# The branch output projections take their PSUM banks from the projections' pair instead of the attention scores' three

## The chip, the cores and the metric

One core of a Trainium2 chip runs the whole program once. The metric is the device time of one execution in microseconds (us); the median of several runs counts.

## The reference, cut to what matters

Two layers of a diffusion backbone work on 256 latent and 256 context tokens of width 1024. In each layer a combined input projection feeds four token mixers (differential attention, a Hyena long convolution, a Conformer convolution, latent attention). Their outputs are projected to the model's width branch by branch, gated and added, and projected once more; a mixture of 16 experts follows.

```python
def merge_branches(ys, g, p):
    gates = jax.nn.sigmoid(g.reshape(*g.shape[:-1], N_BRANCH, D_MODEL))
    acc, start = 0.0, 0
    for i, (y, w) in enumerate(zip(ys, BRANCH_WIDTHS)):
        acc = acc + gates[..., i, :] * (y @ p['w_branch'][start:start + w])
        start += w
    return acc @ p['w_out']
```

The change concerns `y @ p['w_branch']`, one product for each of the four branches. The last layer computes it for the latent tokens alone, so its tiles are 256 wide where those of layer 0 are 512.

## The kernel before

Every product of the mixers is an fp32 product made of three fp32r matmuls (`mm3`, lines 355 to 357): high by high, high by low and low by high parts, all accumulated in one PSUM bank of 128x512 fp32.

The eight banks are dealt out by four small pools. A bank is given to a new tile when all readers of the tile that held it last are done, and TensorE (PE), which works strictly in the order of the program, waits for that at the first matmul of the new tile.

- `pm`, two banks: the input projections with the gates (`body` in `stream`), the output projection, later the experts' first product.
- `psc`, three banks: the attention scores, the branch projections, the Hyena transforms, later the experts' second product.
- `px`, one bank, and `pt`, two banks: attention outputs and transposes.

A generator stands for each strand of work (`stream`, `hyena`, `mla`, `diff`, four `branch` strands, the expert loader). A planner, `Order.run`, records their instructions in one order that it works out from estimated costs. The banks are not part of its estimates. Where a strand yields, another can put its work in between.

Two properties matter here. A projection of the "t" kind, a gate above all, takes its bank once and is accumulated in pieces: in layer 0 of 4 of the 8 steps of k (`PIECE = (4, 2)`: two pieces of 12 matmuls), in layer 1 of 2 steps (four pieces of 6 matmuls). Between the pieces other strands run and the bank stays held. A gate tile is read by ScalarE (ACT), which writes tanh of it to `tg` (line 984).

A `branch` strand makes eight tiles of 128 output columns, two for each 256 columns of weights. A tile is 6 matmuls for three of the branches and 12 for the branch of the differential attention (`nk` is 2 or 4). It is read by VectorE (DVE), which multiplies it by the gate (line 1051 for the first branch that arrives, line 1054 for the others). DVE also works in the order of the program: score maxima (1272), attention weights (1506, 1507), the low parts of weights (349), the Conformer's taps (1230), the modulation's products (521) stand before and after these evictions. A weight's low part on DVE (line 349) waits for its high part, which ACT casts (line 348).

The expert loader issues the weights of the experts (`we`) on the queue of SyncE (SP), each as soon as one of twelve large SBUF buffers is free. The mixers use these buffers as well (`wi` raw weights, `wq` split weights, `uh` and `ul` the tokens), so the loader is held until projections and output projection give them back.

Of the kernel before, what the change touches and what calls it, by code (L numbers as in the profile page):

```python
# [213 lines left out]
def _a(n):  # L214
    return 0.19 + n / 1200


def _d(n):
    return 0.07 + n / 960


def _q(n):
    return 0.1 + n / 480
# [3 lines left out]
def kernel(ctx: ExitStack, tc: tile.TileContext, x, ctxt, cols, skip, lamb, fng, ta, tb, tcn, td,  # L227
# [23 lines left out]
    def ps(tag, bufs):  # L251
        return psum.tile([128, 512], F32, name=tag, tag=tag, bufs=bufs)

    def pm():
        return ps("pm", 2)

    def psc():
        return ps("psc", 3)
# [7 lines left out]
    def big(name, dt=F32):  # L266

        S.used += 1
        assert S.used <= NB, name
        return work.tile([128, 2048], dt, name=name, tag="big", bufs=NB)  # L270
# [4 lines left out]
    def room(n=1, low=False):  # L275
        return lambda: S.used + n + (S.kept if low else 0) <= NB

    def t2(name, dt=F32, w=512):
        return work.tile([128, w], dt, name=name, tag="t2", bufs=NT2)
# [66 lines left out]
    def split(hi, lo, src, eng=nc.vector):  # L346

        nc.scalar.copy(hi, src)  # L348
        eng.tensor_tensor(lo, src, hi.bitcast(F32), op=OP.subtract)  # L349

    def mm3(out, terms, first=True, last=True):

        n = len(terms)
        for i, (lh, ll, rh, rl) in enumerate(terms):
            nc.tensor.matmul(out, lh, rh, start=first and i == 0, stop=False)  # L355
            nc.tensor.matmul(out, lh, rl, start=False, stop=False)  # L356
            nc.tensor.matmul(out, ll, rh, start=False, stop=last and i == n - 1)  # L357
# [39 lines left out]
    def layer(l):  # L397
# [319 lines left out]
        def acc(k):  # L717
            n = len(accs)
            return accs[k % n][:, k // n * TQ:(k // n + 1) * TQ]
# [271 lines left out]
        def two(name):  # L991

            if last:
                t = t2(name + "hl", F32R)
                return t[:, :TQ], t[:, TQ:]
            return t2(name + "h", F32R), t2(name + "l", F32R)

        def branch(i, os, k0, ready, early):
            nk = len(os)
            ws, arr = {}, {}  # L1000

            def load(d2):
                if d2 < 4:
                    ws[d2] = []
                    for k in range(0, nk, 2):
                        w = t2("wbr")
                        nc.sync.dma_start(w.rearrange("p (k c) -> p k c", k=2),
                                          w_branch[l, (k0 + k) * 128:(k0 + k + 2) * 128].rearrange("(k p) c -> p k c", p=128)
                                          [:, :, d2 * 256:(d2 + 1) * 256])
                        ws[d2].append(w)  # L1010
                    arr[d2] = S.load(nk * 0.125)

            def cut(d2):
                bs = []
                for w in ws.pop(d2):
                    hi, lo = t2("wbrh", F32R), t2("wbrl", F32R)
                    split(hi, lo, w)
                    bs.append((hi, lo))
                return bs

            CUT = {"act": nk / 2 * _a(512), "dve": nk / 2 * _d(512)}
            yield early
            for d2 in range(BA[l]):
                load(d2)
            yield ready
            if not accs:
                yield from S.until(room(ns))
                accs.extend(big("acc") for _ in range(ns))
            yield tg_ev[i, 0]
            yield arr[0]  # L1030
            bs = cut(0)
            ready = yield CUT
            for d2 in range(4):
                yield tg_ev[i, 2 * d2]
                yield ready
                load(d2 + BA[l])
                if i == 0 and d2 == 2:
                    br_ev.t = 0.0
                for m in range(2):
                    kd = d2 * 2 + m  # L1040
                    yield tg_ev[i, kd]
                    p = psc()
                    mm3(p[:, :TQ], [tuple(b[:, (k % 2) * 256 + m * 128:(k % 2) * 256 + (m + 1) * 128] for b in bs[k // 2])
                                    + os[k] for k in range(nk)])
                    a = acc(kd)
                    g = tg.pop((i, kd))
                    tg_n[0] -= 1
                    acc_n[kd] += 1
                    PE = {"pe": nk * 3 * TQ * 0.00042, "dve": _d(TQ)}
                    if acc_n[kd] == 1:  # L1050
                        nc.vector.scalar_tensor_tensor(a, g, 1.0, p[:, :TQ], op0=OP.add, op1=OP.mult)
                        yield PE
                    else:
                        nc.vector.scalar_tensor_tensor(g, g, 1.0, p[:, :TQ], op0=OP.add, op1=OP.mult)
                        if acc_n[kd] < 4:
                            nc.gpsimd.tensor_tensor(a, a, g, op=OP.add)
                            yield {**PE, "pool": _q(TQ)}
                        else:
                            nc.vector.tensor_tensor(a, a, g, op=OP.add)
                            yield {**PE, "dve ": _d(TQ)}  # L1060
                    if acc_n[kd] == 4:
                        ac[kd] = two("a")
                        split(ac[kd][0], ac[kd][1], a)
                        acc_ev[kd].t = yield {"act": _a(TQ), "dve": _d(TQ)}
                    if m == 0 and d2 < 3:
                        yield arr[d2 + 1]
                        nxt = cut(d2 + 1)
                        ready = yield CUT
                if d2 < 3:
                    bs = nxt  # L1070
# [547 lines left out]
        if l == 0:  # L1618
            gens += [lambdas(), residual()]
        gens += [hyena(), mla(), rope("k"), rope("q"), diff(),  # L1620
                 branch(1, o_hy, 4, hy_done, k_ev), branch(2, o_cf, 6, cf_done, cfa_ev[1][0]),
                 branch(3, o_ml, 8, ml_done, ml_mid), branch(0, o_df, 0, df_done, df_mid)]
        mv = products([(l, 1), (l, 2)] + ([] if last else [(l + 1, 0)]), (1,) if last else (0, 1), lat_ev if last else u_ev)
        mv_at = MVP[l]
# [518 lines left out]
```

## Time and profile before

| | us |
|---|---|
| median of 3 runs | 1992.57 (1991.23 to 1993.66) |
| the profiled execution, whole | 1990.53 |
| its span in the trace | 1988.7 |
| PE busy | 1699.1 (85%) |
| DVE busy | 974.7 (49%) |
| ACT busy | 461.8 (23%) |
| mean granted clock of TensorE | 0.919 |

The program has four stages: the mixers of layer 0 up to about 660 us, the experts of layer 0 up to about 1130 us, the mixers of layer 1 up to about 1520 us, the experts of layer 1 to the end. The branch projections run from 205.0 to about 604 us and from 1338.3 to about 1484 us. A busy share says little across stages: PE leads in the mixers, the transfers of weights in the experts. Matmuls overlap, so a matmul of 0.39 us (128x512) starts every 0.23 us, and one of 0.28 us (128x256) every 0.12 us.

### The profile page before, as it was taken

The numbers are of one execution on the slowest core, as the hardware profiler recorded it, in microseconds if no ns is written. First come the engines' busy times: TensorE is split into PE (matmuls) and PEld (weight loads), VectorE is DVE, ScalarE is ACT, GpSimd is POOL, SyncE is SP. The second block draws the span as 40 slices with busy tenths as digits, with TensorE's granted clock in tenths as the row PEclk, the third lists the DMA queues.
The fourth block names the chain that finished last, engine by engine and source line by source line (L and its number), as shares of the span: only waits on it lengthen the run. The fifth ranks groups of instructions, "written<-read, shape, count | busy, mean of one in ns | idle before, by whom it ended". The sixth has DMA issues, their size and how long they took to land.

```text
span 1988.7 us, 27943 instructions
## 1 busy us (share of the span) xinstructions
PE 1699.1 (85%) x11132; PEld 1101.6 (55%) x11132; DVE 974.7 (49%) x2057; ACT 461.8 (23%) x933; POOL 219.7 (11%) x229
## 2 busy tenths in 40 slices
PE   5899999888989799899898788998997767767665
PEld 2677788666769634343332277888986423322222
DVE  4787789877774311222332285887864111111012
ACT  4423233334332100010100163344442000000001
POOL 1332021031101000000000042410210000000000
PEclk9899999899989899999999998999998977777677
DMA  8525334422436799999999944565659999999997
GB/s 282 169 86 167 128 117 134 148 90 85 133 128 241 277 381 413 416 417 416 414 417 415 393 149 154 176 197 167 209 208 367 413 415 414 412 414 412 414 414 274
DMA packets 206554, 550.72 MB, mean 277 GB/s; under 512 B 14102, under 2 KB 94168, under 8 KB 176600
## 3 DMA queue, kind: packets, MB, share of 16 engines
q1 hardware_dynamic: 206424, 548.94, 73.4%
q8 instruction: 88, 1.44, 0.3%
q14 instruction: 42, 0.34, 0.0%
HBM read 547.83 MB, written 1.05 MB: 276 GB/s over the span
## 4 chain that ended last, share of the span: by engine, by line
PE 50%; DMA 27%; DVE 12%; issue 6%; ACT 4%; POOL 1%; SPq 1%; ACTq 0%; DVEq 0%; POOLq 0%
DMA we<-in_w_ei_dram 13%; PE pm L1963 11%; DMA we<-in_w_eo_dram 8%; PE pm L355 7%; PE pm L357 7%; PE pm L356 7%; PE psc L1988 4%; DMA h<-in_w_eo_dram 3%; DVE wq L349 2%; PE psc L1852 2%; PE psc L355 2%; PE psc L357 2%; PE psc L356 1%; DVE aw L521 1%; DMA h<-in_w_ei_dram 1%
## 5 line engine op out<-in xcount | busy, mean ns | idle before, releaser
L1963 PE MATMUL pm<-we,xe 128*32 128x256 f32 (+1 forms) x2912 | 402.7, 537 | 101.2 <-DMA we<-in_w_ei_dram 99.4
L1963 PEld LDWEIGHTS pm<-we,xe 128*32 128x32 f32 (+1 forms) x2912 | 135.3, 135 | 346.2 <-issue 183.0
L355 PE MATMUL pm<-uh,wq 128*128 128x256 f32 (+1 forms) x832 | 290.8, 349 | 2.2 <-ACT u L819 1.9
L356 PE MATMUL pm<-ul,wq 128*128 128x256 f32 (+1 forms) x832 | 281.5, 338 | 1.0 <-POOL ul L828 1.0
L357 PE MATMUL pm<-uh,wq 128*128 128x256 f32 (+1 forms) x832 | 281.1, 338 | 0.0
L1975 DVE SCALAR_TENSOR_TENSOR ea<-ea,pm 128x512 f32<-128x512 f32 (+1 forms) x32 | 17.7, 554 | 428.5 <-ACT ea L1974 428.5
L349 DVE TENSOR_TENSOR wq<-wi,wq 128x1024 fp32r<-128x1024 f32 x131 | 166.9, 1285 | 78.7 <-ACT wq L348 78.3
L1988 PE MATMUL psc<-we,eaT 128*32 128x256 f32 (+1 forms) x1280 | 172.1, 513 | 34.2 <-DMA we<-in_w_eo_dram 34.2
L355 PEld LDWEIGHTS pm<-uh,wq 128*128 128x128 f32 x832 | 161.0, 193 | 23.9 <-issue 5.2
L356 PEld LDWEIGHTS pm<-ul,wq 128*128 128x128 f32 x832 | 161.2, 194 | 17.4 <-POOL ul L828 1.2
L357 PEld LDWEIGHTS pm<-uh,wq 128*128 128x128 f32 x832 | 160.8, 193 | 16.5
L2000 DVE TENSOR_TENSOR ye<-psc,modr 32x512 f32<-32x512 f32 (+1 forms) x120 | 66.4, 553 | 202.1 <-PE psc L1988 200.7
L348 ACT CAST wq<-wi 128x1024 fp32r<-128x1024 f32 x132 | 136.1, 1043 | 11.7 <-DMA wi<-in_w_in_dram 10.3
L1988 PEld LDWEIGHTS psc<-we,eaT 128*32 128x32 f32 (+1 forms) x1280 | 58.9, 130 | 141.9 <-issue 75.7
L1974 ACT ACTIVATE ea<-pm 128x512 f32<-128x512 f32 (+1 forms) x32 | 15.7, 491 | 482.2 <-PE pm L1963 482.2
L1230 DVE SCALAR_TENSOR_TENSOR ca<-up,colt,ca 128x510 f32<-128x510 f32 (+29 forms) x120 | 81.0, 675 | 2.2
L2032 ACT COPY eaT<-pt 128x512 f32<-128x512 f32 (+1 forms) x32 | 15.3, 479 | 277.7 <-PE pt L2030 277.7
L521 DVE SCALAR_TENSOR_TENSOR aw<-aw,h 128x512 f32<-128x512 f32 x96 | 77.4, 807 | 3.4
L1276 ACT ACTIVATE e<-psc,nm 128x512 f32<-128x512 f32 (+1 forms) x72 | 44.4, 618 | 147.7 <-DVE nm L1274 145.5
L355 PE MATMUL pm<-wq,uh 128*128 128x256 f32 (+1 forms) x240 | 71.7, 299 | 4.4 <-DVE rsq L319 1.6
L356 PE MATMUL pm<-wq,uh 128*128 128x256 f32 (+1 forms) x240 | 69.6, 290 | 0.0
L357 PE MATMUL pm<-wq,ul 128*128 128x256 f32 (+1 forms) x240 | 69.6, 290 | 0.0
(409 smaller groups left out, 2646.3 us busy)
## 6 DMA issues: line engine op xcount, KB each, us to landing
we<-in_w_ei_dram SPq DMA_DIRECT2D x233, 1024.0 KB, 14.3
we<-in_w_eo_dram SPq DMA_DIRECT2D x110, 1024.0 KB, 14.6
wi<-in_w_in_dram SPq DMA_DIRECT2D x58, 1024.0 KB, 5.4
aw<-in_ada_t_dram SPq DMA_DIRECT2D x160, 256.0 KB, 5.4
we<-in_w_ei_dram SPq DMA_DIRECT2D x52, 256.0 KB, 8.1
wbr<-in_w_branch_dram SPq DMA_DIRECT2D x40, 256.0 KB, 5.6
h<-in_w_ei_dram SPq DMA_DIRECT2D x40, 256.0 KB, 16.3
h<-in_w_eo_dram SPq DMA_DIRECT2D x40, 256.0 KB, 16.2
```

The lines of the kernel that those rows point to most:

```text
L348: nc.scalar.copy(hi, src)
L349: eng.tensor_tensor(lo, src, hi.bitcast(F32), op=OP.subtract)
L355: nc.tensor.matmul(out, lh, rh, start=first and i == 0, stop=False)
L356: nc.tensor.matmul(out, lh, rl, start=False, stop=False)
L357: nc.tensor.matmul(out, ll, rh, start=False, stop=last and i == n - 1)
L521: nc.vector.scalar_tensor_tensor(o, wt_, 1.0, cb[s, k], op0=OP.mult, op1=OP.mult, accum_out=ends[lm, g][0][:, s, c, k:k + 1])
L1230: nc.vector.scalar_tensor_tensor(o, up[:, :, max(d, 0):256 + min(d, 0)], cw[:, c0 + d:c0 + d + 1], o, op0=OP.mult, op1=OP.add)
L1276: nc.scalar.activation(e, p[:, :nk], AF.Exp, scale=scale, bias=nm, accum_out=s)
L1852: nc.tensor.matmul(p[:, kk * n:(kk + 1) * n], h[2 * s + b][k // 4][:, (k % 4) * 128:(k % 4 + 1) * 128], hot[:, 2 * i + b], start=b == 0, s ...
L1963: nc.tensor.matmul(dst[j * M:(j + 1) * M, :], lhs, w[o + j * FW // 512][:, j * FW % 512:j * FW % 512 + FW], start=k == 0, stop=k == KC - 1 ...
L1988: nc.tensor.matmul(py[j * M:(j + 1) * M, :FW], aT[:, c * 128 + q * M:c * 128 + (q + 1) * M], w[f % 2 * 2 + j * FW // 512][:, j * FW % 512: ...
L2000: nc.vector.tensor_tensor(ye[eg][s][c0 // 512][e4 * CAP:(e4 + 1) * CAP, c0 % 512:c0 % 512 + FW], py[r0:r0 + CAP, :FW], mod5[r0:r0 + CAP, c ...
```

## The change

One line in `branch` asks the other pool for the tile:

```diff
-                    p = psc()
+                    p = pm()
                     mm3(p[:, :TQ], [tuple(b[:, (k % 2) * 256 + m * 128:(k % 2) * 256 + (m + 1) * 128] for b in bs[k // 2])
                                     + os[k] for k in range(nk)])
```

The planner does not know of banks, so every engine's instructions stand in the order in which they stood. What differs is the tile that 480 matmuls (64 tiles of 6 or 12) write and their evictions read, and with it who waits for whom. PE in the tail of layer 1's mixers, before; the names end in tile numbers, `pm_11817` is a gate in its pieces, `psc_11840` and `psc_11849` are tiles of two branches:

```order
L357 MATMUL pm_11817<-uh_7856,wq_11550 128x256
L355 MATMUL psc_11840<-ohl_11516,wbrh_11754 128x256
L356 MATMUL psc_11840<-ohl_11516,wbrh_11754 128x256
L357 MATMUL psc_11840<-ohl_11516,wbrl_11755 128x256
L355 MATMUL psc_11840<-ohl_11527,wbrh_11754 128x256
L356 MATMUL psc_11840<-ohl_11527,wbrh_11754 128x256
L357 MATMUL psc_11840<-ohl_11527,wbrl_11755 128x256
L355 MATMUL psc_11849<-ohl_9732,wbrh_11674 128x256 [waits DVE_49]
```

The same place with the change, where the waits are those for the banks' last readers:

```order
L357 MATMUL pm_11817<-uh_7856,wq_11550 128x256
L355 MATMUL pm_11840<-ohl_11516,wbrh_11754 128x256 [waits Activation_49]
L356 MATMUL pm_11840<-ohl_11516,wbrh_11754 128x256
L357 MATMUL pm_11840<-ohl_11516,wbrl_11755 128x256
L355 MATMUL pm_11840<-ohl_11527,wbrh_11754 128x256
L356 MATMUL pm_11840<-ohl_11527,wbrh_11754 128x256
L357 MATMUL pm_11840<-ohl_11527,wbrl_11755 128x256
L355 MATMUL pm_11849<-ohl_9732,wbrh_11674 128x256 [waits DVE_49]
```

No instruction moved. The gate `pm_11817` is open across both tiles and holds one bank of the pair, so `pm_11840` has to wait for the other one, which ACT reads as the gate before it, and `pm_11849` for DVE's eviction of `pm_11840`. Before, `psc_11849` waited for the eviction of a tile three places back.

## Rows read from the trace of the kernel before

**Rows 1.** The page's first line.
```profile
span 1988.7 us, 27943 instructions
```
**Rows 2.** Windows: stretch, its length, busy PE PEld DVE ACT POOL, PEclk, DMA share, GB/s.
```profile
330.00:605.00 275.00, 243.73 (x1182) 191.63 (x1181) 210.49 (x466) 98.10 (x196) 39.67 (x38) 0.93 0.38 124
605.00:660.00 55.00, 55.00 (x472) 55.00 (x472) 19.77 (x43) 12.76 (x37) 9.98 (x14) 1.00 0.55 198
660.00:1130.00 470.00, 428.69 (x2002) 167.36 (x2003) 125.62 (x248) 39.50 (x80) 8.02 (x11) 0.97 1.01 405
1333.00:1420.00 87.00, 79.61 (x613) 75.08 (x612) 72.06 (x146) 41.26 (x78) 10.80 (x12) 0.96 0.60 192
1444.00:1486.00 42.00, 38.58 (x314) 37.57 (x313) 28.67 (x52) 18.61 (x35) 7.67 (x10) 1.00 0.50 173
1520.00:1985.00 465.00, 322.08 (x3340) 138.45 (x3340) 69.44 (x170) 22.36 (x58) 3.69 (x4) 0.77 0.99 399
```
**Rows 3.** Waits of PE, 320 to 605 us: total, times, longest.
```profile
PE psc L355 <- ACT e L1276: 8.4, 4, 6.2
```
**Rows 4.** Waits of PE, 1333 to 1486 us: total, times, longest.
```profile
PE psc L355 <- ACT e L1276: 6.1, 2, 3.1
```
**Rows 5.** Matmuls on branch weights: count, ns min/median/max, first and last start, forms.
```profile
L355 PE MATMUL psc<-oh,wbrh x80: 389/389/795, 205.0 to 603.5; 128*128 128x512 f32 x80
L355 PE MATMUL psc<-ohl,wbrh x80: 278/283/387, 1338.3 to 1483.8; 128*128 128x256 f32 x80
```
**Rows 6.** Timeline at 490 us, PE, ACT, DVE: start, us, idle before.
```profile
490.33 0.50 PE L355 MATMUL psc<-oh,wbrh 128*128 128x512 f32 x1 [0.64 <-ACT e L1276]
...
489.50 0.69 ACT L1276 ACTIVATE e<-psc,nm 128x512 f32<-128x512 f32 x1 [4.45 <-DVE nm L1274]
...
490.11 0.68 DVE L1054 SCALAR_TENSOR_TENSOR tg<-tg,psc 128x512 f32<-128x512 f32 x1
```
**Rows 7.** Timeline at 254 us, PE and ACT.
```profile
253.74 0.39 PE L355 MATMUL pm<-uh,wq 128*128 128x512 f32 x1
...
254.21 0.59 ACT L984 ACTIVATE tg<-pm 128x512 f32<-128x512 f32 x1
```
**Rows 8.** Timeline at 526 us, PE and DVE.
```profile
525.57 0.39 PE L355 MATMUL pm<-uh,wq 128*128 128x512 f32 x1
...
528.56 0.68 DVE L1054 SCALAR_TENSOR_TENSOR tg<-tg,psc 128x512 f32<-128x512 f32 x1
```
**Rows 9.** Timeline at 1340 us, PE and ACT.
```profile
1339.76 0.28 PE L355 MATMUL pm<-uh,wq 128*128 128x256 f32 x1
...
1342.03 0.38 ACT L984 ACTIVATE tg<-pm 128x256 f32<-128x256 f32 x1
```
**Rows 10.** Timeline at 1360 us, PE and DVE.
```profile
1359.30 0.28 PE L355 MATMUL pm<-uh,wq 128*128 128x256 f32 x1
...
1363.24 0.39 PE L355 MATMUL psc<-ohl,wbrh 128*128 128x256 f32 x1 [3.06 <-ACT e L1276]
...
1363.08 0.41 DVE L1051 SCALAR_TENSOR_TENSOR acc<-tg,psc 128x256 f32<-128x256 f32 x1
```
**Rows 11.** Timeline at 1474 us, PE, DVE, ACT.
```profile
1474.04 0.28 PE L355 MATMUL psc<-ohl,wbrh 128*128 128x256 f32 x1
...
1476.36 0.69 DVE L349 TENSOR_TENSOR wbrl<-wbr,wbrh 128x512 fp32r<-128x512 f32 x1
1476.97 0.75 DVE L1054 SCALAR_TENSOR_TENSOR tg<-tg,psc 128x256 f32<-128x256 f32 x2
```
**Rows 12.** Windows behind the wait of 3.06 us, columns as in rows 2.
```profile
1363.00:1365.00 2.00, 1.76 (x12) 1.76 (x13) 1.96 (x6) 1.99 (x6) 0.00 (x0) 0.86 0.01 3
1365.00:1368.00 3.00, 3.00 (x16) 3.00 (x16) 2.16 (x4) 0.83 (x3) 0.00 (x0) 0.52 0.33 87
```
**Rows 13.** Waits of SP's queue, 590 to 670 us.
```profile
SPq L1690 <- PE pm L357: 23.2, 4, 12.6
```
**Rows 14.** Waits of SP's queue, 1470 to 1530 us.
```profile
SPq L1690 <- PE pm L357: 19.2, 5, 6.2
```

## The prediction

> **What bounds the kernel now.** I read the windows first, stage by stage, then PE's waits, then the timeline where the branch projections stand. PE leads in both mixer stages: it is busy 243.7 of the 275 us up to 605 us, 79.6 of 87 us from 1333 us and 38.6 of 42 us from 1444 us, while DVE is busy 210.5, 72.1 and 28.7 us of these [rows 2]. In the two expert stages the transfers lead: a DMA share of 1.01 over 470 us and 0.99 over 465 us [rows 2]. Before each of these stages the share is only 0.55 and 0.50 [rows 2], because the expert loader's issues wait for PE's last reads of the mixers' buffers [rows 13, 14]. So a microsecond that PE loses in a mixer stage starts the stream of expert weights a microsecond later, and a stream at a share of 1 has nothing with which to catch up. The question is what PE loses or gains between 205 and 605 us and between 1333 and 1486 us.
>
> **What falls away.** No instruction is added, removed or moved on any queue, SP's and POOL's among them. The branch tiles leave the three score banks, and the waits for those banks go. PE waits for the exponentials of score tiles 8.4 us in four places of layer 0 and 6.1 us in two of layer 1 [rows 3, 4]. That is the most that can be gained, 14.5 us, if nothing took their place.
>
> **What comes in.** A gate holds one of the two banks over all its pieces, with branch tiles put in between; these then share the single bank left, and a tile must wait until DVE or ACT has read its predecessor. A branch tile passes quickly: six matmuls at a start every 0.23 us are 1.4 us in layer 0, at 0.12 us 0.7 us in layer 1 (the matmuls themselves last 0.389 and about 0.283 us and overlap [rows 5]). The eviction itself takes 0.4 to 0.7 us, but stands in DVE's queue behind other work. So I set, for each tile of the pair in the new deal of banks, the end of the predecessor's reader in this trace against the tile's own start. PE takes up a released bank 0.14 us after the reader's end: the exponential ends at 489.50 + 0.69 = 490.19 and PE starts at 490.33 [rows 6]. With that, 53 of the 134 tiles in the three stretches would start too early: 14 in layer 0 by 14.8 us together, 19 between 1333 and 1420 us by 31.6 us, 20 between 1444 and 1486 us by 36.8 us. Five show the kinds:
>
> - At 490.33 us the second tile of a pair follows its gate's first piece. It waited for the exponential until 490.19; now for DVE's eviction of the first tile, which ends at 490.11 + 0.68 = 490.79 [rows 6]. One wait replaces another, 0.6 us longer. This recurs at 502.07 us, and longer at 477.05 us.
> - At 253.74 us a gate gets the bank of the gate before last, which ACT reads until 254.21 + 0.59 = 254.80 [rows 7]: 1.2 us.
> - At 525.57 us a gate follows a branch tile whose eviction ends at 528.56 + 0.68 = 529.24 [rows 8]: 3.8 us.
> - At 1339.76 us a gate needs what ACT reads until 1342.03 + 0.38 = 1342.41 [rows 9]: 2.8 us.
> - At 1474.04 us a tile needs the bank that DVE frees behind a weight's low part, 1476.97 plus about 0.41, so 1477.38 [rows 11]: 3.5 us.
>
> The ends of the cost: if every eviction moved on rigidly with PE, each overshoot would be paid in full and the sum would be 14.8 + 31.6 + 36.8 = 83 us. If no eviction moved at all, only the largest of each stretch would be paid, 3.8 at 525.57, 4.3 at 1359.30 and 3.8 at 1478.40 us: 12 us, less waits that shrink. Neither holds: an eviction moves by as much as the work for which its queue waited had moved, and often this work lies before the stall. So I carried the delay on, stall by stall, along the waits of the program, each eviction kept at its distance behind the latest thing it waited for in the trace.
>
> *Layer 0*, nine places: 1.2 (253.74), 1.3 (397.65), 0.5 (466.16), 1.5 (477.05), 0.65 twice (490.33, 502.07), 1.4 (515.71), 2.8 (525.57), less 0.85 of a wait on a transpose bank soon behind it that shrinks, and 1.0 (578.70). Sum 10.2 us. A further 0.6 at 411 us is given back at 424 us, where PE waits for something else.
>
> *Layer 1, 1333 to 1420 us*: 2.9 (1339.76), 0.8, 0.7, 2.8 (1359.30), 1.0 (1376.84), 0.2, 1.5, 2.2, 0.7, 0.7, together 13.5. The stall at 1359.30 us, where the bank is free only at 1363.08 + 0.41 = 1363.49 [rows 10], lies right before a wait of 3.06 us that ended with an exponential [rows 10]; this wait vanishes and three small ones shrink behind the new stalls, which gives back 5.1. Net 8.4 us.
>
> *Layer 1, 1444 to 1486 us*: 0.9, 2.0, 1.7, 1.8, 1.1, 2.4 (1474.04), 0.2, 1.8 and some smaller ones, together 12.3; waits for weights' low parts and the one ahead of the output projection shrink by 4.0. Net 8.3 us.
>
> The sum is 10.2 + 8.4 + 8.3 = 26.9 us, against ends of 12 and 83. It is nearer to the lower end because most banks are freed behind work that does not depend on the stalled tile, as at 1474 us.
>
> **A rule weighed against the rows.** The wait of 3.06 us at 1363 us [rows 10] left its mark on the clock: granted 0.86 in the two microseconds behind it and 0.52 in the three after that [rows 12], so mostly the lower level, 1.2 of 2.4 GHz; that took 0.14 x 2 + 0.48 x 3 = 1.7 us. The Trainium skill, TensorE: Matmul & The Clock Gate, section "A second HAM failure mode: psum-queue depth-cycling", reports of a kernel that went round its PSUM banks and idled shortly between groups of matmuls that its clock kept switching, which cost throughput. By the rows no stall under 3 us is priced so, and the sum stays 26.9. By that rule the new stalls would each be followed by a slow stretch; the trace before cannot show it, and it is a rival below.
>
> **The rivals.** *The clock falls too.* If each of the 15 or so stalls of 1 us and more were followed by a slow stretch of 1.7 us [rows 12], 25 us more; if only the four of about 2.4 us and more, 7 us: 1990.5 + 26.9 + 7 = 2024, plus the 2 us below, 2026. For it: the stalls are close to each other in the tail of layer 1. Against: the clock stood at 1.00 over 1444 to 1486 us [rows 2], though PE idled 3.4 us there. The section of the Trainium skill named above is the rule of this rival. *The stream of weights takes it up.* If the loader's issues did not wait for the mixers' end, the expert stages would hide what layer 0 loses, and the time would be some 2009. Against: rows 13 and 14. *It gets faster.* The exponential waits go (14.5 us) and the evictions come before the exponentials that they follow now: 1992.6 - 14.5 = 1978. It decides at 490 us: the eviction would have to end before 490.19; it stands behind the second maximum and ends at 490.79 [rows 6]. *Nothing changes*, since evictions that are late here come in time once PE is a little later: 1992.6. Against: the nine places of layer 0 are each a wait for DVE or ACT work that begins after PE has delivered, so it moves with PE. That the change does not do what it says can be left out: the order of instructions shows all 64 tiles in the other pool.
>
> **How the numbers follow.** The profiled execution took 1990.53 us (a span of 1988.7 us [rows 1] and 1.8 us around it); 1990.5 + 26.9 = 2017.4. The median of the three runs is 2.0 us above it, so 2019. A measurement of this kernel can tell about 0.2%, 4 us, from no change. Chances: this forecast 0.72, within some 8 us either way for the carrying (2011 to 2027); the clock 0.12 (2024 to 2044); hidden in part 0.08 (2000 to 2010); nothing 0.03; faster 0.05. The range runs from 2007 to 2029: it leaves out the last two cases, most of the hidden one and the upper part of the clock's. Slower by over 0.2%: 0.92; within: 0.03; faster: 0.05.
>
> **What would show it.** In the profile of the changed kernel PE's waits for exponentials at the branch projections are gone or nearly so, and waits of line 355 for `tg` of lines 1054 and 984 stand in their place, some 40 to 55 us in all. The output projection of layer 0 begins about 10 us later, that of layer 1 about 27 us later; the expert stages last as long as before, at the same DMA share. Wrong would be the sum if the waits came to less than 25 us, the carrying if the delay at 605 us were under 6 or over 15 us, and the passing on if an expert stage were shorter.

## The result and the profile after

The changed kernel takes 2020.1 us (median of five runs, 2017.3 to 2023.0) against 1991.2 us for the kernel before in the same session (1987.2 to 1993.7): a ratio of 1.0146, 95% interval [1.0131, 1.0161], so 26 to 32 us slower. The forecast was 2019, from a sum of 26.9 us. The profiled execution of after took 2019.85 us, and its span is 29.4 us longer than before's. The page's first line and its line of engines:

```profile
span 2018.1 us, 27921 instructions
PE 1708.7 (85%) x11132; PEld 1104.9 (55%) x11132; DVE 972.7 (48%) x2057; ACT 463.0 (23%) x933; POOL 217.5 (11%) x229
```

The five engines have as many working instructions as before (PE 11132); the total is lower by 22, all of them instructions that only wait for semaphores. The span grew, and the next rows say where. They are the groups of branch matmuls by form, the counterpart of [rows 5]: count, ns min/median/max, first and last start in us, shape.

```profile
L355 PE MATMUL pm<-oh,wbrh x80: 389/395/796, 206.4 to 615.3; 128*128 128x512 f32 x80
L355 PE MATMUL pm<-ohl,wbrh x80: 277/283/582, 1350.4 to 1516.5; 128*128 128x256 f32 x80
```

The four starts are 1.4, 11.8, 12.1 and 32.7 us later than in [rows 5]. From the first to the last branch tile layer 0 lost 10.4 us. Between the layers, where the experts of layer 0 run, the delay stayed nearly as it was (11.8, then 12.1), and layer 1 added 20.6 us, of which 1.3 came back right behind the last tile, in a wait ahead of the output projection that shrank. So 31.3 us were left there; 29.4 stood at the end, since 1.9 us came back in the experts of layer 1. The first 1.4 us lie ahead of every instruction that the change touches. PE's matmuls stand in the same order in both traces, so each start can be set against its counterpart's; that is what "start by start" means below, and a delay is the difference of the two.

The windows of after; the columns are those of [rows 2]. The first four begin and end where PE stands at the counterpart of the matmul at which a window of [rows 2] begins and ends. The fifth lies in the second expert stage.

```profile
332.94:616.80 283.86, 244.36 (x1182) 191.23 (x1181) 209.96 (x466) 98.42 (x196) 39.50 (x38) 0.94 0.37 120
671.80:1140.92 469.12, 430.34 (x2002) 167.02 (x2003) 125.59 (x248) 39.51 (x80) 8.03 (x11) 0.96 1.01 406
1345.07:1441.06 95.99, 82.32 (x613) 76.59 (x612) 73.08 (x149) 41.75 (x78) 11.42 (x14) 0.95 0.55 174
1465.09:1518.64 53.55, 42.30 (x314) 40.56 (x313) 29.24 (x53) 18.81 (x35) 7.62 (x10) 0.94 0.41 135
1552.00:2014.43 462.43, 320.16 (x3340) 137.60 (x3340) 68.62 (x167) 22.36 (x58) 4.14 (x4) 0.77 1.00 400
1477.00:1480.00 3.00, 3.00 (x14) 3.00 (x15) 0.84 (x2) 0.38 (x1) 0.65 (x1) 0.50 0.55 189
1480.00:1484.00 4.00, 4.00 (x24) 4.00 (x23) 0.84 (x2) 0.43 (x3) 0.74 (x1) 0.62 0.00 0
1392.20:1394.20 2.00, 1.95 (x9) 1.96 (x10) 0.27 (x1) 0.48 (x2) 0.00 (x0) 0.50 0.00 0
1394.20:1398.00 3.80, 3.80 (x21) 3.80 (x21) 2.46 (x5) 1.32 (x2) 0.00 (x0) 0.53 0.00 0
1423.80:1428.00 4.20, 4.16 (x24) 4.16 (x25) 3.93 (x7) 1.52 (x2) 0.73 (x1) 0.65 0.43 147
1354.50:1358.00 3.50, 3.47 (x29) 3.47 (x30) 2.79 (x6) 1.44 (x2) 0.00 (x0) 1.00 0.42 119
```

The three mixer stretches (first, third, fourth row) are 8.9, 9.0 and 11.6 us longer than in [rows 2]. PE's busy time in them grew by 0.6, 2.7 and 3.7 us: most of the loss is waiting, and in layer 1 a part is PE's own time at a lower clock. The expert stages (second and fifth row) have the same DMA share as before; the first is within 1 us as long. The last six rows are read below.

PE's waits at line 355, from 205 to 615 us (the first two rows) and from 1343 to 1520 us (the last three): us in total, times, longest.

```profile
PE pm L355 <- DVE tg L1054: 16.5, 8, 7.8
...
PE pm L355 <- ACT tg L984: 1.7, 2, 0.9
...
PE pm L355 <- DVE tg L1054: 11.9, 8, 2.7
PE pm L355 <- DVE acc L1051: 6.8, 3, 4.0
PE pm L355 <- ACT tg L984: 6.2, 6, 2.5
```

No row names the exponentials of line 1276 any more, where [rows 3, 4] have 8.4 and 6.1 us. In their place stand 18.2 us of waits for gate and branch evictions in layer 0 and 24.9 us in layer 1: 43.1 in all. Less the 14.5 that went, that is 28.6 us more. It is not yet the balance: in layer 1 the waits for the weights' parts went as well. Before, from 1333 to 1486 us, they were:

```profile
PE psc L357 <- DVE wbrl L349: 3.3, 5, 1.2
PE psc L355 <- ACT wbrh L348: 1.4, 3, 0.7
```

That leaves some 24 us of waits more. Start by start it is the same: the starts whose wait changed moved by 9.5 us net in layer 0 and by 7.1 and 7.1 in the two stretches of layer 1, 23.7 in all. Another 6.0 us (0.9, 1.9 and 3.2) were lost between them, while PE ran.

The longest one shows the kind. Timeline of after at 483 us, PE and DVE: start, duration, and in brackets the idle time and its releaser; then four stalls of layer 1.

```profile
483.72 0.80 PE L355 MATMUL pm<-oh,wbrh 128*128 128x512 f32 x1 [7.81 <-DVE tg L1054]
...
482.20 0.68 DVE L1272 TENSOR_REDUCE mx<-psc 128x1 f32<-128x512 f32 x1
482.92 0.15 DVE L1274 TENSOR_SCALAR nm<-mx 128x1 f32<-128x1 f32 x1
482.99 0.68 DVE L1054 SCALAR_TENSOR_TENSOR tg<-tg,pm 128x512 f32<-128x512 f32 x1
...
1354.53 0.39 PE L355 MATMUL pm<-uh,wq 128*128 128x256 f32 x1 [2.55 <-ACT tg L984]
...
1392.25 0.58 PE L355 MATMUL pm<-ohl,wbrh 128*128 128x256 f32 x1 [4.05 <-DVE acc L1051]
...
1423.84 0.39 PE L355 MATMUL pm<-uh,wq 128*128 128x256 f32 x1 [1.75 <-ACT tg L984]
...
1476.99 0.55 PE L355 MATMUL pm<-ohl,wbrh 128*128 128x256 f32 x1 [2.74 <-DVE tg L1054]
```

Before, PE stood here for 6.21 us until an exponential freed a score bank. Now it stands for 7.81, until DVE's eviction of the pair's first tile ends at 482.99 + 0.68 = 483.67; that eviction is in order behind a row maximum of the scores and its negation, so the tile still waits for the softmax, only one step later in it. One wait took the place of another, 1.6 us longer.

### The profile page after: what moved, and what is told of

The parts are those of the page before. It is cut to its first block, busy times and chain, and to the rows that moved or that the text cites. A ratio compares the mean times of both kernels' runs of the same rounds, so it can differ in the third digit from the quotient of the medians.

```text
span 2018.1 us, 27921 instructions
## 1 busy us (share of the span) xinstructions
PE 1708.7 (85%) x11132; PEld 1104.9 (55%) x11132; DVE 972.7 (48%) x2057; ACT 463.0 (23%) x933; POOL 217.5 (11%) x229
## 4 chain that ended last, share of the span: by engine, by line
PE 50%; DMA 26%; DVE 14%; issue 5%; ACT 4%; SPq 1%; POOL 1%; ACTq 0%; DVEq 0%; POOLq 0%
DMA we<-in_w_ei_dram 14%; PE pm L1963 11%; PE pm L355 8%; PE pm L357 8%; PE pm L356 8%; DMA we<-in_w_eo_dram 5%; PE psc L1988 5%; DVE wq L349 3%; DMA h<-in_w_eo_dram 2%; PE psc L1852 2%; DMA h<-in_w_ei_dram 2%; DVE aw L521 1%; ACT wq L348 1%; DMA aw<-in_ada_w_dram 1%; DVE aj L521 1%
## 5 line engine op out<-in xcount | busy, mean ns | idle before, releaser
L1963 PE MATMUL pm<-we,xe 128*32 128x256 f32 (+1 forms) x2912 | 409.6, 546 | 98.4 <-DMA we<-in_w_ei_dram 96.6
```

The source lines that it names most:

```text
L1963: nc.tensor.matmul(dst[j * M:(j + 1) * M, :], lhs, w[o + j * FW // 512][:, j * FW % 512:j * FW % 512 + FW], start=k == 0, stop=k == KC - 1 ...
```

## The experiments

Each edit is against the kernel before. Gains and losses in us are the ratio times the median before of its own session (1990 to 1992 us), with its interval. Figures by stretch come from one profiled execution each.

**Layer 0 alone, layer 1 alone.** Do the two layers cost what the sum says, and do they add?

```diff
-                    p = psc()
+                    p = pm() if l == 0 else psc()
```

> Branch tiles take the pair of banks in layer 0 alone. Theory (PE waits for late evictions of the bank that an open gate leaves over, and the delay passes through the expert stage unshortened): 10.2 us slower than before, 1991.2 + 10.2 = 2001.4, all of it in nine waits between 250 and 600 us; the output projection of layer 0 begins 10 us later and everything behind it by the same. Rival (the stream of expert weights takes up what layer 0 loses): about 1991 to 1994. Rival (the clock falls behind the new stalls): over 2006.

Measured: 2001.6 us, 1.0053 [1.0033, 1.0073], so +10.6 us (7 to 15). The branch groups of this kernel:

```profile
L355 PE MATMUL pm<-oh,wbrh x80: 389/389/796, 205.1 to 614.2; 128*128 128x512 f32 x80
L355 PE MATMUL psc<-ohl,wbrh x80: 278/283/582, 1349.5 to 1495.0; 128*128 128x256 f32 x80
```

Delays against [rows 5]: 0.1, 10.7, 11.2, 11.2. All of it is lost in layer 0's mixers, nothing is given back over the 730 us behind them, and layer 1, left alone, adds nothing.

```diff
-                    p = psc()
+                    p = pm() if l == 1 else psc()
```

> Branch tiles take the pair of banks in layer 1 alone. Theory: 16.7 us by the sum, 18 to 19 with the slow stretch of the clock that the changed kernel showed behind its stall of 2.7 us in the tail, so 2008 to 2010; together with the run for layer 0 alone it adds up to the whole change, 29. If the two layers were not independent (the clock, the transfers), the two runs would miss that sum by more than 4 us.

Measured: 2007.6 us, 1.0088 [1.0065, 1.0111], so +17.5 us (13 to 22). In the trace the first branch tile of layer 1 starts 0.8 us late and the last one 20.1 us late. The two halves give 10.6 + 17.5 = 28.1 us, the whole change 29.1 by its ratio: they add within the noise.

**A delay without any change of banks.** The prediction rests on a delay at the end of a mixer stage being paid in full, since the stream of expert weights starts later. This kernel keeps the three banks and puts 24 matmuls that nothing reads ahead of each output projection; in the profile each matmul shows as two halves.

```diff
+                p = pm()
+                for n in range(24):
+                    nc.tensor.matmul(p[:, :256], ident, tat[:, :256], start=n == 0, stop=n == 23)
                 for q in range(4):
```

> The kernel before, with 24 fp32 matmuls of 128x256 in front of each layer's output projection whose result nobody reads; at 0.43 us each (three such matmuls of the latent attention's values start at 181.95, 182.38 and 182.82 us) they hold PE for 10.4 us per layer, 20.7 us in all, at places where no bank is short. Theory (time that PE loses in a mixer stage is paid in full, since the loader waits for the output projection): 20 to 21 us slower, about 2012. Rival (the expert stages, bound by transfers, hide it): 1991 to 1996. In between: the expert stages come out shorter than 470 and 465 us.

Measured: 2009.9 us, 1.0101 [1.0079, 1.0122], so +20.1 us (16 to 24). Its timeline (start, duration) at the added matmuls and at the loader:

```profile
606.42 10.61 PE L963 MATMUL pm<-tat 128*128 128x256 f32 x48
...
649.21 7.24 SPq L1693 DMA_DIRECT2D we<-in_w_ei_dram  x3
```

10.6 us were put in. The second row of the timeline is an issue of expert weights by the loader on SP's queue; before it starts at 638.28:

```profile
638.28 5.80 SPq L1690 DMA_DIRECT2D we<-in_w_ei_dram  x2
```

It moved by 10.9 us, with the mixers' end. Layer 1's branch tiles start 10.2 us late, so at most 0.7 us of the delay was hidden. The rival that the stream of weights takes it up falls.

**The tail of layer 1.** By the sum, 8.3 us are lost between 1444 and 1486 us, where branch 2 is projected. Its tiles alone stay with the scores here:

```diff
-                    p = psc()
+                    p = psc() if i == 2 else pm()
```

> The change for three branches; the Conformer's branch stays with the scores' three banks. Theory (a tile waits because the tile just before it used the one bank that is left): between 1444 and 1486 us only the tiles of the Conformer's and the differential attention's branch alternate, so with one of them elsewhere nearly all of that stretch's cost goes, from 8.3 (10 with the clock) to 0.5 us; layer 0 costs 3.5 instead of 10.2, 1333 to 1420 us still 8.3. In all 12.3 us, about 2003.5. Rival (each branch tile in the pair has a price of its own, 29 us over 64 tiles, 0.45 each): 48 tiles, 22 us, about 2013, and half of the tail's cost stays.

Measured: 2003.0 us, 1.0066 [1.0045, 1.0087], so +13.1 us (9 to 17). PE's longest waits from 1445 to 1505 us:

```profile
PE pm L355 <- ACT tg L984: 1.8, 3, 1.0
PE pm L355 <- DVE tg L1054: 1.3, 2, 1.1
```

No other wait there is over 0.8 us. Set start by start against the trace before, PE loses 0.4 us in the tail, with 8.9 us still lost between 1333 and 1420 us and 5.5 in layer 0, where 3.5 were expected. So the tail's loss belongs to branch 2's tiles, as the sum has it.

**Gates where the branches were.** Is it the third bank that counts, or which tiles share? Here the two change places: the branch tiles go to the pair and the gates, in their stead, to the scores' banks. So the branch tiles have two banks with no gate beside them, and gates share three with the scores.

```diff
-                            p = pm()
+                            p = psc() if fn is gate_out else pm()
...
-                    p = psc()
+                    p = pm()
```

> The branch tiles take the pair of banks as in the change, but the gates, whose tiles stay open over two or four pieces, move to the scores' three banks. Theory (it is the open gate that leaves one bank): with the gates elsewhere the branch tiles have both banks of the pair between the projections that remain; PE's waits of the tail fall from 10 to about 2.5 us, those of 1333 to 1420 us vanish, layer 0 costs 5.6 us because gates and scores now crowd three banks. In all 7.8 us, about 1999.5. Rival (a pair is too small for the branch tiles whether a gate is open or not): it stays near 2018 to 2020.

Measured: 2004.0 us, 1.0060 [1.0036, 1.0083], so +11.9 us (7 to 17). PE's waits from 100 to 615 us (first row) and from 1333 to 1530 us:

```profile
PE psc L355 <- ACT e L1276: 7.5, 4, 3.6
...
PE psc L355 <- ACT e L1276: 6.3, 4, 2.8
PE pm L355 <- DVE tg L1054: 4.9, 4, 2.9
```

The waits for exponentials are back, now ahead of gates. The loss is under half of the change's and far from the rival's 2018 to 2020, which fits a cost that comes mostly from a gate held open beside the branch tiles in two banks. The expected 7.8 us lie just inside the interval. In the profiled execution, the slowest of the four, 4.2 of its 18.1 us extra had been lost by the first branch tile, 3.5 of them ahead of the first moved gate, which starts at 189.6 us. The three stretches lost 7.4, -1.7 and 3.9 us, 9.6 together, and 3.0 more went between 605 and 1300 us, where neither gates nor branch tiles run. Of layer 0's 7.4 us only some 1.4 are waits that grew; the rest was lost while PE ran, more of its time at the lower clock than before.

**Only the pair's second tile in the two banks.** The pair is then split over both pools.

```diff
-                    p = psc()
+                    p = pm() if m else psc()
```

> Of each two tiles of 128 columns of a branch the first stays with the scores' banks and only the second takes the pair's. Theory: the second tile no longer waits for the first one's eviction behind it in one bank, nor for an exponential; in layer 0 a gain of 1.8 us, from 1333 to 1420 us a loss of 3.9, in the tail of 1.6. In all 3.7 us, about 1995.5, where half of the change's price would be 14 us, about 2006 (rival: a price per tile).

Measured: 2001.0 us, 1.0056 [1.0034, 1.0078], so +11.1 us (7 to 16); a miss, by 3 us at least. Three stalls of its timeline, then the windows behind them and one in the tail:

```profile
527.30 0.80 PE L355 MATMUL pm<-uh,wq 128*128 128x512 f32 x1 [4.72 <-DVE tg L1054]
...
1381.04 0.58 PE L355 MATMUL pm<-uh,wq 128*128 128x256 f32 x1 [2.92 <-DVE acc L1051]
...
1411.47 0.58 PE L355 MATMUL pm<-uh,wq 128*128 128x256 f32 x1 [3.38 <-ACT tg L984]
```

```profile
527.30:530.00 2.70, 2.70 (x6) 2.15 (x7) 2.67 (x5) 1.58 (x4) 1.60 (x1) 0.50 0.00 0
...
1381.00:1385.00 4.00, 3.96 (x18) 3.96 (x19) 2.69 (x5) 1.35 (x4) 0.00 (x0) 0.50 0.00 0
1385.00:1388.00 3.00, 3.00 (x20) 3.00 (x18) 0.02 (x1) 1.38 (x3) 0.00 (x0) 0.65 0.00 0
...
1411.50:1414.00 2.50, 2.50 (x12) 2.50 (x12) 2.30 (x3) 0.85 (x1) 0.73 (x1) 0.50 0.62 214
...
1487.00:1490.00 3.00, 3.00 (x18) 3.00 (x17) 1.39 (x4) 1.62 (x3) 0.00 (x0) 0.58 0.83 210
```

Each is a gate's wait for the eviction of a branch tile or for ACT's read of the gate before it. Behind each of the three the granted clock is 0.50, the lower level. By the clocks that is 1.4 + 2.0 + 1.1 + 1.3 + 1.3 = 7.1 us of PE's time in the five rows. The kernel before has slow stretches too, those of [rows 12], one around 477 us and this one:

```profile
1378.00:1382.00 4.00, 4.00 (x23) 4.00 (x22) 2.98 (x6) 1.44 (x4) 0.00 (x0) 0.57 0.00 0
```

Start by start this kernel lost 0.6, 6.2 and 2.9 us in the three stretches, 9.7 in all, where -1.8, 3.9 and 1.6 were expected. Half of PE's busy time at the lower level, which is what that level costs, comes to 10.5 us in layer 0 (10.7 before), 6.2 from 1333 to 1420 us (3.4 before) and 1.7 in the tail (none before). In layer 1 these 4.5 us cover the miss of 3.6. In layer 0 they do not, and its miss of 2.4 us is open: the wait of 6.2 us at 477 us vanished, but only 2.5 us of that were left by 490 us, and the stall of 4.72 us came later. Whether the stalls brought the slow stretches is not shown either (see the last section). Why the median is 1.4 us above the 9.7 was not traced.

**Better than both.** If waits for exponentials cost 14.5 us before and a shared pair costs more, the tiles should go where banks stand free. The pair's second tile goes to the two banks of the transposes, except in the last branch:

```diff
-                    p = psc()
+                    p = pt() if m and i != 3 else psc()
```

> The second tile of each two takes a bank of the transposes' pool (two banks, emptied by a copy that stands right behind its transposes), in all branches but that of the latent attention, whose tiles all stay with the scores. Theory: the second tile waits neither for an exponential that reads a score bank (14.5 us in six places before) nor for an open gate; a gain of 5.2 us in layer 0 and 5.5 us from 1333 to 1420 us, nothing in the tail, so 10.7 us faster than before, about 1981. Rival (the waits for exponentials are only put off, because the strands wait for each other anyway): within 3 us of before.

Measured: 1982.5 us (ten runs), 0.9957 [0.9939, 0.9974], so 8.6 us less than before (5 to 12): faster than both kernels. PE's waits from 330 to 615 us:

```profile
PE psc L355 <- ACT wbrh L348: 11.9, 3, 6.7
...
PE psc L357 <- DVE wbrl L349: 2.6, 2, 1.5
...
PE psc L355 <- ACT e L1276: 1.0, 1, 1.0
```

From 1333 to 1490 us no row names the exponentials. So of the 14.5 us of waits for them [rows 3, 4] 1.0 is left. Not all of it is gained: the wait of 6.2 us at 477 us goes, and PE's start moves forward by 6.4 us; then a tile comes before its weight's low part is ready and waits 1.1 us for that, and 4.4 of the 6.4 are lost again by 490 us. In the profiled execution, one of the slower of the ten, layer 0 gained 1.6 us (5.2 expected), the stretch from 1333 to 1420 us 5.6 (5.5), and the tail lost 1.5 (0). Of the 5.6 about half is waiting; the rest is the clock, which stood at 1.00 over that whole stretch, where before it had two slow stretches of 1.7 us.

## Why the prediction was right, step by step

- **What falls away.** The waits for exponentials went completely, as said, and gave back little: five of the six places got a longer wait, and at the sixth, at 1363 us, a new stall of 2.37 us stands just ahead.
- **Layer 0**, forecast 10.2: the change alone gave 10.4 (11.8 less the 1.4 ahead of it), layer 0 by itself 10.6. The places agree singly; PE's start against the trace before, forecast and measured: 1.2 and 1.1 at 253.74; 1.3 and 1.3 at 397.65; 1.5 and 1.6 at 477.05; 0.65 and 0.5 at 490.33; 2.8 and 2.4 at 525.57; 1.0 and 1.0 at 578.70. Net, the changed waits gave 9.5; 0.9 was lost between them.
- **Layer 1, 1333 to 1420**, forecast 8.4: measured 9.0, with 2.7 at 1339.76 (2.9 forecast), 2.5 at 1359.30 (2.8) and the vanishing wait of 3.06 us giving back 3.2. The agreement is in part luck: the changed waits gave 7.1 net, 1.3 less than forecast, and 1.9 were lost while PE ran, for which the sum had nothing.
- **Layer 1, 1444 to 1486**, forecast 8.3: measured 10.2, the term that was most too small. 2.3 at 1474.04 (2.4) and 1.7 at 1478.40 (1.8) came as said. The changed waits gave 7.1 net, again less than forecast; 3.2 were lost while PE ran. The step that failed is the clock, put at nothing with the words "by the rows no stall under 3 us is priced so": behind the stall of 2.74 us at 1476.99 the clock was 0.50 for 3 us and 0.62 for 4, which is 0.5 x 3 + 0.38 x 4 = 3.0 us of PE's time. Before, the tail stood at 1.00 [rows 2]. The rows shown were too few for these words: in the trace before PE also waited 2.26 us ahead of 548.46 us, and from 548.5 to 552 us the clock was 0.52.
- **The clock as a rival.** It was right in a small part. The stall of 4.05 us at 1392.25, forecast as 1.0 us on top of the second wait for exponentials of 3.1 us [rows 4], was followed by 0.50 for 2 us and 0.53 for 3.8; that of 1.75 us at 1423.84 by 0.65 for 4.2; that of 2.55 us at 1354.53 by 1.00. With the tail's 3.0 us that makes 1.0 + 1.8 + 1.5 + 3.0 = 7.3 us of PE's time at the lower level, against two stretches of 1.7 us before. So 3.9 us were new, neither the 7 nor the 25 us of the rival. In layer 1's two terms the waits came out 2.5 us below the forecast and 5.1 us were lost while PE ran, most of it to the clock: two errors that partly cancelled, so that the terms were only 2.5 us too small.
- **What a stall costs in clock.** The prediction put 1.7 us of lower clock down to the wait of 3.06 us [rows 10, 12]. The other runs do not bear that out as a price of the stall; the rows are in the last section.
- **Passing on.** Nearly in full, as forecast: 11.8 us behind layer 0's mixers, 12.1 us ahead of layer 1's; the delay put in by hand shows the same without any bank in play. Behind layer 1's mixers 31.3 us stood (about 27 were forecast at the output projection), of which the last expert stage gave back 1.9.
- **The check on the waits.** 40 to 55 us of waits for `tg` were forecast. Waits for `tg` come to 36.3 us; with those for `acc` of line 1051, which evicts the first branch's tiles and was left out there, they are 43.1.
- **What the sum leaves over.** The sum was 26.9 and the spans differ by 29.4. The three terms measured 10.4 + 9.0 + 10.2 = 29.6; the 1.4 us ahead of the first branch tile add to that, and the 1.9 us given back at the end nearly cancel them. For the 1.4: PE's granted clock over the first 205 us is 0.95 in after, 0.97 before, in code that is the same in both:

```profile
0.00:205.00 205.00, 170.38 (x834) 122.28 (x835) 148.54 (x288) 75.96 (x136) 51.39 (x51) 0.95 0.51 174
```

```profile
0.00:205.00 205.00, 169.78 (x838) 122.14 (x839) 150.48 (x294) 75.96 (x136) 51.42 (x51) 0.97 0.52 174
```

The kernel with the second tile in the transposes also has 0.95 there, and the two kernels with layer 0 or a delay changed start their first branch tile within 0.4 us of before's. So it differs between executions of the same code; what sets it was not looked into.

## What to carry to other kernels

Count the accumulations that are open at once, not the banks: a pool of two in which one tile stays open over other work is a pool of one for everything else. Which wait frees a bank matters as much as how many there are; an eviction that stands in order behind a softmax waits for the softmax too. To price a smaller pool, deal its banks anew over the old trace, tile by tile, and carry each delay on with the evictions held to what they wait for: here that put the waits at 26.9 us where 23.7 came. Then allow for the clock, which here took some 4 us more in layer 1, at places that another execution of the same code need not share.

## What the runs showed of the hardware

The stalls repeat from one kernel to the next, the slow stretches of the clock do not. In the kernel with layer 0 alone changed, layer 1's mixers are those of before, and the branch tile of [rows 10] waits 3.06 us again. Before, the clock behind it was 0.86 and then 0.52 [rows 12]; here it is 1.00 (first two rows). Yet in the tail, where the clock stood at 1.00 before and no wait is over 1.2 us, this kernel has a slow stretch (third row). In the kernel with layer 1 alone changed, the tail's stall comes again, 2.73 us long. In after the clock behind it was 0.50 to 0.62; here it is 1.00 (last two rows).

```profile
1374.42 0.39 PE L355 MATMUL psc<-ohl,wbrh 128*128 128x256 f32 x1 [3.06 <-ACT e L1276]
...
1374.40:1378.40 4.00, 3.98 (x33) 3.98 (x34) 3.75 (x8) 3.22 (x7) 0.00 (x0) 1.00 0.28 70
...
1464.90:1468.30 3.40, 3.40 (x18) 3.40 (x18) 2.08 (x5) 0.41 (x1) 0.73 (x1) 0.50 0.69 237
...
1466.59 0.36 PE L355 MATMUL pm<-ohl,wbrh 128*128 128x256 f32 x1 [2.73 <-DVE tg L1054]
...
1466.60:1473.60 7.00, 6.16 (x48) 5.89 (x48) 3.32 (x6) 2.25 (x4) 1.39 (x2) 1.00 0.21 70
```

So the length of a stall does not tell whether the clock falls behind it. Differences of this size (1.7 to 3 us) are for medians, not for one trace; what decides them was not found.
